# Sliding windows: partition order batch and half, alternating halves, one queue for all stores

## The chip, the cores and the metric

One core of a Trainium2 chip runs the kernel. The metric is the device time of one execution in microseconds.

## The reference

```python
batch, c, h, w = (16, 64, 64, 64)        # x, float32; window_size 8, stride 4
n_h = n_w = (64 - 8) // 4 + 1            # 15
for i in range(n_h):
    for j in range(n_w):
        result[:, i, j] = x[:, :, i*4 : i*4+8, j*4 : j*4+8]
```

The result has the shape (16, 15, 15, 64, 8, 8). Nothing is calculated: 16.78 MB are read from HBM, and 58.98 MB are written, because windows overlap by half in both directions.

## The kernel before

The rows of an image are cut into four bands of 16 (`HQ`, index q), the channels into two halves of 32 (`CH`, index ch). The whole input is held in SBUF in one tile `L`, 128 partitions by 32 channels, 16 rows and 64 columns. The partition is 32·q + 2·batch + ch.

Sixteen loads of 1 MB (line 50) fill it: four chunks of eight channels, in each the four bands, each band on 32 neighbouring partitions. Bands 0 and 1 are loaded by SP's queue, bands 2 and 3 by ACT's.

Then, for each column j of the 15 window columns and each slot s of 4 window rows in a band, VectorE gathers into a tile `g` what the four bands need for window row i = 4·q + s. For s = 0, 1, 2 the windows lie inside a band, and one copy of 128 x 2048 elements does it (line 66). For s = 3 the window's lower half is in the next band: one copy of 128 x 1024 takes the upper halves (line 68), and three copies of 32 x 1024 take the first rows of the band below, from the next 32 partitions (line 70). Then each band's 32 partitions are stored by a DMA of 256 KB (line 77), bands 0 and 1 on SP, 2 and 3 on ACT. Window row 15 doesn't exist, so SP stores 8 rows for each column and ACT 7. The pool has nine buffers for `g`. The first window (j = 0, s = 0) is made and stored in four chunks of channels.

The engines take their instructions in program order. The framework adds the waits: a copy waits for the loads that it reads, and for the stores of the buffer that it reuses; a store waits for the copies of its tile. Eight DMA completion semaphores are used in turn, so that the issue of a DMA also waits for the one that had the same semaphore, the eighth before it in the program.

Of the kernel before, what the change touches and what calls it, by code (L numbers as in the profile page):

```python
# [1 line left out]

# [4 lines left out]


@with_exitstack  # L10
def kernel(
    ctx: ExitStack,
    tc: tile.TileContext,
    x: bass.AP,
    window_size: int,
    stride: int,
    out: bass.AP,
):
    nc = tc.nc
    P = nc.NUM_PARTITIONS  # L20

    B, C, H, W = x.shape
    Bo, NH, NW, Co, WSo, WSo2 = out.shape
    WS = int(window_size)
    ST = int(stride)
    assert Bo == B and Co == C and WSo == WS and WSo2 == WS

    f32 = mybir.dt.float32

    HQ = 4  # L30
    CH = P // (B * HQ)
    CL = C // CH
    RB = H // HQ
    Q = P // HQ
    NSLOT = RB // ST
    assert Q == 32 and WS == 2 * ST

    lpool = ctx.enter_context(tc.tile_pool(name="lpool", bufs=1))
    gpool = ctx.enter_context(tc.tile_pool(name="gpool", bufs=9))


    L = lpool.tile([P, CL, RB, W], f32)
    x_v = x.rearrange("b (ch cl) (hq r) w -> hq (b ch) cl (r w)", ch=CH, hq=HQ)
    o_v = out.rearrange("b i j (ch cl) r w -> i j b ch (cl r w)", ch=CH)
    queues = [nc.sync, nc.sync, nc.scalar, nc.scalar]
    NCH = 4
    cw = CL // NCH
    for k in range(NCH):
        for q in (0, 2, 1, 3):
            queues[q].dma_start(  # L50
                out=L[q * Q : (q + 1) * Q, k * cw : (k + 1) * cw, :, :],
                in_=x_v[q, :, k * cw : (k + 1) * cw, :],
            )

    CFREE = CL * WS * WS
    for j in range(NW):
        cols = slice(j * ST, j * ST + WS)
        for s in range(NSLOT):
            g = gpool.tile([P, CL, WS, WS], f32, name="g")
            chunks = NCH if j == 0 and s == 0 else 1  # L60
            n = CL // chunks
            last = s == NSLOT - 1
            for k in range(chunks):
                cs = slice(k * n, (k + 1) * n)
                if not last:
                    nc.vector.tensor_copy(out=g[:, cs, :, :], in_=L[:, cs, s * ST : s * ST + WS, cols])  # L66
                else:
                    nc.vector.tensor_copy(out=g[:, cs, 0:ST, :], in_=L[:, cs, s * ST : RB, cols])  # L68
                    for q in range(HQ - 1):
                        nc.vector.tensor_copy(  # L70
                            out=g[q * Q : (q + 1) * Q, cs, ST:WS, :],
                            in_=L[(q + 1) * Q : (q + 2) * Q, cs, 0:ST, cols],
                        )
                for q in (0, 2, 1, 3):
                    i = NSLOT * q + s
                    if i < NH:
                        queues[q].dma_start(  # L77
                            out=o_v[i, j, :, :, k * CFREE // chunks : (k + 1) * CFREE // chunks],
                            in_=g[q * Q : (q + 1) * Q, cs, :, :],
                        )  # L80


# [1 line left out]
_INS = ['x', 'window_size', 'stride']  # L84
_OUTS = [((16, 15, 15, 64, 8, 8), 'float32')]

_NUMBERS = {'window_size': 8, 'stride': 4}


# [26 lines left out]
```

## Time and profile before

| | us |
|---|---|
| Median of 3 runs | 248.83 |
| Lowest and highest run | 240.36 and 253.69 |
| Profiled execution | 246.83 |
| Its span in the profile | 245.1 |
| VectorE busy | 96.0 |

The profile gives for each engine the busy time, and for the DMA the busy share of the 16 engines and the rate in slices of the span (40 slices of 6.13 us). q1 is SP's queue and q10 is ACT's. "SPq" and "ACTq" are the issues of DMAs on these queues. The stretches that matter here are the loads (about 2 to 55 us), the stores of both queues (62 to 219 us) and the end, in which only one queue has work. The largest waits of VectorE are for stores that have to free a buffer, 60.5 us at line 66 and 22.0 us at line 68.

### The profile page before, as it was taken

To read this page: it belongs to the slowest core of one execution; us is meant where nothing else is said; L and a number is where in the kernel's file an instruction comes from. 1 tells how busy PE (TensorE), PEld (TensorE's weight loads), DVE (VectorE), ACT (ScalarE), POOL (GpSimd) and SP (SyncE) were. 2 spreads that over 40 slices of the span, in tenths; PEclk is the share of its full clock that TensorE was granted. 3 is DMA by queue.
4 is the path that set the end of the run, shared out by engine and by line. 5 is a ranking of instruction groups with operands and counts; after the bars stand their busy time and mean duration, and the time that the engine had idled before them with its cause. 6 is when DMAs were issued, how large, how long until landed. Compare 5 with 4: busy or idle time off the path is not lost.

```text
span 245.1 us, 659 instructions
## 1 busy us (share of the span) xinstructions
DVE 96.0 (39%) x108; POOL 0.2 (0%) x4
## 2 busy tenths in 40 slices
DVE  0000000008996646453726454545555554542000
POOL 0000000000000000000000000000000000000000
DMA  6999999997999999999999999999999999999996
GB/s 212 317 320 318 318 318 320 322 326 184 326 346 314 332 321 322 330 308 328 342 333 326 322 333 338 325 338 336 308 350 350 336 345 309 326 341 272 211 210 142
DMA packets 15733, 75.82 MB, mean 309 GB/s; under 512 B 4048, under 2 KB 4048, under 8 KB 8656
## 3 DMA queue, kind: packets, MB, share of 16 engines
q1 hardware_dynamic: 8224, 39.85, 51.5%
q10 hardware_dynamic: 7504, 35.92, 43.7%
q14 instruction: 5, 0.04, 0.0%
HBM read 16.78 MB, written 58.98 MB: 309 GB/s over the span
## 4 chain that ended last, share of the span: by engine, by line
DMA 74%; DVE 7%; SPq 5%; ACTq 2%; issue 1%; DVEq 0%
DMA out_dram<-g 53%; DMA L<-in_x_dram 22%; SPq L77 5%; DVE g L70 4%; DVE g L66 3%; ACTq L77 1%; DVE g L68 1%; ACTq L50 1%; DVEq L111 0%; DVEq L66 0%; DVEq L68 0%
## 5 line engine op out<-in xcount | busy, mean ns | idle before, releaser
L66 DVE COPY g<-L 128x2048 f32<-128x2048 f32 (+1 forms) x48 | 55.1, 1159 | 103.1 <-DMA out_dram<-g 60.5
L70 DVE COPY g<-L 32x1024 f32<-32x1024 f32 x45 | 30.8, 684 | 1.1
L68 DVE COPY g<-L 128x1024 f32<-128x1024 f32 x15 | 10.4, 692 | 22.0 <-DMA out_dram<-g 22.0
L97 POOL MEMSET const-bfloat16-1.0<- 128x1 bf16 x1 | 0.1, 102 | 0.0
L97 POOL MEMSET const-uint8-127<- 128x1 uint8 x1 | 0.1, 102 | 0.0
L97 POOL MEMSET const-float32-0.0<- 128x1 f32 x1 | 0.1, 99 | 0.2 <-issue 0.2
L97 POOL MEMSET const-float32-1.0<- 128x1 f32 x1 | 0.1, 99 | 0.0
## 6 DMA issues: line engine op xcount, KB each, us to landing
out_dram<-g SPq DMA_DIRECT2D x118, 256.0 KB, 5.9
out_dram<-g ACTq DMA_DIRECT2D x103, 256.0 KB, 6.1
L<-in_x_dram SPq DMA_DIRECT2D x8, 1024.0 KB, 26.2
L<-in_x_dram ACTq DMA_DIRECT2D x8, 1024.0 KB, 26.1
out_dram<-g SPq DMA_DIRECT2D x8, 64.0 KB, 2.1
out_dram<-g ACTq DMA_DIRECT2D x8, 64.0 KB, 2.1
```

Of the source, the lines that this page charges most:

```text
L50: queues[q].dma_start(out=L[q * Q : (q + 1) * Q, k * cw : (k + 1) * cw, :, :], in_=x_v[q, :, k * cw : (k + 1) * cw, :],)
L66: nc.vector.tensor_copy(out=g[:, cs, :, :], in_=L[:, cs, s * ST : s * ST + WS, cols])
L68: nc.vector.tensor_copy(out=g[:, cs, 0:ST, :], in_=L[:, cs, s * ST : RB, cols])
L70: nc.vector.tensor_copy(out=g[q * Q : (q + 1) * Q, cs, ST:WS, :], in_=L[(q + 1) * Q : (q + 2) * Q, cs, 0:ST, cols],)
L77: queues[q].dma_start(out=o_v[i, j, :, :, k * CFREE // chunks : (k + 1) * CFREE // chunks], in_=g[q * Q : (q + 1) * Q, cs, :, :],)
L97: nc = _bacc.Bacc("TRN2", target_bir_lowering=False, num_devices=1)
```

## The change

The partition is now 64·ch + 4·batch + q: the two channel halves lie on the two halves of the partitions, and the bands of one image on neighbours.

A load takes one half, one band and eight channels: 16 partitions, every fourth one, 512 KB. All loads are on ACT's queue. The very first piece is cut in two by batches 0 to 7 and 8 to 15; after it two pieces of half 1 and two of half 0 take turns.

All stores are on SP's queue. A store of a window inside a band takes all four bands of one half at once: 64 partitions, 512 KB (`store`, line 90). A window across two bands is stored by `store_x` (line 96): 16 partitions, every fourth one, for two columns together. The windows across bands are made in a tile `gx` by one copy of 128 x 1024 (line 83) and one `stream_shuffle` of 128 x 1024 (line 84), which gives each partition the first rows of the next partition.

The order: window column 14 (`J`), slot 0 and its crossing windows are made first, and of these half 0 is stored, batches 0 to 7 and then 8 to 15. Then seven pairs of columns follow. For each pair, the crossing windows are made first; then, slot by slot, the windows of both columns are made, and half 1 is stored (two `store`, one `store_x`), then half 0. The rest of column 14 comes last. `g` has five buffers, `gx` has two, each for two columns.

```diff
-    gpool = ctx.enter_context(tc.tile_pool(name="gpool", bufs=9))
+    gpool = ctx.enter_context(tc.tile_pool(name="gpool", bufs=5))
+    xpool = ctx.enter_context(tc.tile_pool(name="xpool", bufs=2))
...
-    queues = [nc.sync, nc.sync, nc.scalar, nc.scalar]
-    for k in range(NCH):
-        for q in (0, 2, 1, 3):
-            queues[q].dma_start(
-                out=L[q * Q : (q + 1) * Q, k * cw : (k + 1) * cw, :, :],
-                in_=x_v[q, :, k * cw : (k + 1) * cw, :],
-            )
+    def load(ch, q, k, b0=0, nb=B):
+        cs = slice(k * cw, (k + 1) * cw)
+        p0 = ch * HP + b0 * HQ + q
+        nc.scalar.dma_start(
+            out=L[p0 : p0 + (nb - 1) * HQ + 1 : HQ, cs, :, :],
+            in_=x_v[ch, q, b0 : b0 + nb, cs, :],
+        )
+    pieces = [(q, k) for k in range(NCH) for q in range(HQ)]
+    load(0, *pieces[0], 0, HB)
+    load(0, *pieces[0], HB, HB)
+    for n in range(0, len(pieces), 2):
+        for u in pieces[n : n + 2]:
+            load(1, *u)
+        for u in pieces[n + 1 : n + 3]:
+            load(0, *u)
+    nxt = [min(p + 1, 31) for p in range(32)]
+    def window(j, s):
+        g = gpool.tile([P, CL, WS, WS], f32, name="g")
+        cols = slice(j * ST, j * ST + WS)
+        nc.vector.tensor_copy(out=g[:, :, :, :], in_=L[:, :, s * ST : s * ST + WS, cols])
+        return g
+    def crossing(js):
+        g = xpool.tile([P, 2, CL, WS, WS], f32, name="gx")
+        for n, j in enumerate(js):
+            cols = slice(j * ST, j * ST + WS)
+            nc.vector.tensor_copy(out=g[:, n, :, 0:ST, :], in_=L[:, :, (NSLOT - 1) * ST : RB, cols])
+            nc.vector.stream_shuffle(out=g[:, n, :, ST:WS, :], in_=L[:, :, 0:ST, cols], mask=nxt)
+        return g
+    def store(g, ch, j, s, b0=0, nb=B):
+        p0 = ch * HP + b0 * HQ
+        o = o_v[ch, s::NSLOT, j].rearrange("q b f -> b q f")[b0 : b0 + nb]
+        nc.sync.dma_start(out=o, in_=g[p0 : p0 + nb * HQ].rearrange("p c r w -> p (c r w)"))
+    def store_x(g, ch, js, q, b0=0, nb=B):
+        p0 = ch * HP + b0 * HQ + q
+        o = o_v[ch, q * NSLOT + NSLOT - 1, js[0] : js[-1] + 1].rearrange("j b f -> b j f")[b0 : b0 + nb]
+        i = g[p0 : p0 + (nb - 1) * HQ + 1 : HQ, 0 : len(js)].rearrange("p j c r w -> p j (c r w)")
+        nc.sync.dma_start(out=o, in_=i)
+    J = NW - 1
+    g0, gx = window(J, 0), crossing([J])
+    for b0 in (0, HB):
+        store(g0, 0, J, 0, b0, HB)
+        store_x(gx, 0, [J], 0, b0, HB)
+    for j in range(0, J, 2):
+        js = [j, j + 1]
+        gx = crossing(js)
+        for s in range(NSLOT - 1):
+            gs = [window(u, s) for u in js]
+            for ch in (1, 0):
+                for u, g in zip(js, gs):
+                    store(g, ch, u, s)
+                store_x(gx, ch, js, s)
+    gx = crossing([J])
+    gs = [window(J, s) for s in range(NSLOT - 1)]
+    for ch, ss in ((1, (0, 1)), (0, (1, 2)), (1, (2,))):
+        for s in ss:
+            store(gs[s], ch, J, s)
+            store_x(gx, ch, [J], s)
```

More of the change, by code (lines that the diff above doesn't have):

```diff
@@ L33 @@
     RB = H // HQ
-    Q = P // HQ
     NSLOT = RB // ST
-    assert Q == 32 and WS == 2 * ST
+    CFREE = CL * WS * WS
+    HB = B // 2
+    HP = P // CH
+    assert HQ == 4 and CH == 2 and WS == 2 * ST and HP == B * HQ
     lpool = ctx.enter_context(tc.tile_pool(name="lpool", bufs=1))
-    gpool = ctx.enter_context(tc.tile_pool(name="gpool", bufs=9))
+    gpool = ctx.enter_context(tc.tile_pool(name="gpool", bufs=5))
+    xpool = ctx.enter_context(tc.tile_pool(name="xpool", bufs=2))
     L = lpool.tile([P, CL, RB, W], f32)
-    x_v = x.rearrange("b (ch cl) (hq r) w -> hq (b ch) cl (r w)", ch=CH, hq=HQ)
@@ L44 @@
-    o_v = out.rearrange("b i j (ch cl) r w -> i j b ch (cl r w)", ch=CH)
-    queues = [nc.sync, nc.sync, nc.scalar, nc.scalar]
+    x_v = x.rearrange("b (ch cl) (hq r) w -> ch hq b cl (r w)", ch=CH, hq=HQ)
     NCH = 4
     cw = CL // NCH
-    for k in range(NCH):
-        for q in (0, 2, 1, 3):
-            queues[q].dma_start(
-                out=L[q * Q : (q + 1) * Q, k * cw : (k + 1) * cw, :, :],
-                in_=x_v[q, :, k * cw : (k + 1) * cw, :],
-            )
-    CFREE = CL * WS * WS
@@ L56 @@
-    for j in range(NW):
-        cols = slice(j * ST, j * ST + WS)
[L58 to L80, printed above, removed]
@@ new lines @@
+    o_v = out.rearrange("b i j (ch cl) r w -> ch i j b (cl r w)", ch=CH)
+    nxt = [min(p + 1, 31) for p in range(32)]
+    def window(j, s):
+        g = gpool.tile([P, CL, WS, WS], f32, name="g")
+        cols = slice(j * ST, j * ST + WS)
+        nc.vector.tensor_copy(out=g[:, :, :, :], in_=L[:, :, s * ST : s * ST + WS, cols])
[7 more added lines that the diff above has]
+        return g
```

## The prediction

> **What bounds the kernel now.** I read the busy rows first, then the rate of the transfers in stretches, then the waits.
>
> The page's first two sections show which resource is full.
>
> ```profile
> DVE 96.0 (39%) x108; POOL 0.2 (0%) x4
> DMA  6999999997999999999999999999999999999996
> GB/s 212 317 320 318 318 318 320 322 326 184 326 346 314 332 321 322 330 308 328 342 333 326 322 333 338 325 338 336 308 350 350 336 345 309 326 341 272 211 210 142
> q1 hardware_dynamic: 8224, 39.85, 51.5%
> q10 hardware_dynamic: 7504, 35.92, 43.7%
> HBM read 16.78 MB, written 58.98 MB: 309 GB/s over the span
> ```
>
> VectorE works 96 of 245.1 us; the DMA row is at nine tenths nearly throughout. So the time is bytes over rate, and the rate has levels. The last slices stand at 210 with the DMA row as full as before. The answer by stretch gives each level a figure (columns: length, DVE, POOL, clock, DMA share, GB/s):
>
> ```profile
> 2.00:55.00 53.00, 1.28 (x3) 0.00 (x0) 1.00 1.02 319
> 55.00:62.00 7.00, 5.92 (x8) 0.00 (x0) 1.00 0.80 210
> 62.00:219.00 157.00, 86.03 (x94) 0.00 (x0) 1.00 0.95 330
> 226.00:240.00 14.00, 0.00 (x0) 0.00 (x0) 1.00 0.99 210
> ```
>
> Loads take 53 us at 319, stores 157 us at 330, and the end runs at 210 with the DMA share at 0.99. Who works at the end is seen in the DMA view of that window:
>
> ```profile
> q1 hardware_dynamic: 569, 3.12, 98.6%
> out_dram<-g SPq DMA_DIRECT2D x13, 256.0 KB, 4.8
> ```
>
> Only SP's queue is left: bands 0 and 1, which lie on partitions 0 to 63. The engines aren't idle; each packet takes longer. The packet records of the trace say by how much: an 8 KB store packet takes 309 ns at its shortest, which is also the commonest value (26.5 GB/s an engine, 424 for 16); in the last 17 us nearly all take 595 to 639 ns, twice that, and one 256 KB store follows the other every 1.235 us, which is 617 ns a packet. While both queues work, the packets are a mixture, mean about 375. The completion writes of the last stores come in couples within about 20 ns of each other and keep so over 14 stores[...].
>
> [...]
>
> **The change, part by part.**
> Partition order. Partition is now 64·half + 4·batch + band. A full store takes 64 partitions of one half[...]. That is the configuration of the last 17 us of before. [...] batches 0 to 7 and then 8 to 15 of the first pieces go to engines 0 to 7 alone, and then the halves alternate in groups. So the question is how large the lead is when the alternation starts.
>
> Loads. ACT issues all 33. Engines 0 to 7 get two times 8 packets of 4 KB ahead of the rest. In before a load packet took 159 ns in the first 2 us and then mostly 200 to 205 (319 GB/s is 205). From 1.75 us, the first packet of before, the 16 packets end at 4.3 to 5.0. The third load, by before's issue spacing of 0.46 to 0.50 us, starts at about 2.7 on engines 8 to 15. Their lead is 1.6 to 2.3 us, 10 to 11 of the 16 packets of a group[...]. (10.5·205 + 5.5·309)/16 = 241 ns; if the read side runs on meanwhile, 205. I take 225. Engines 0 to 7 have 264 packets: 59.4 us, ending at 61.2. Bounds: 159 ns gives 43.7, wholly in lockstep 309 gives 83.3; before ended at 54.9. Eight transfers may be under way, so no wait is added here.
>
> Start of the stores. DVE runs in program order. It waits for all loads (0.85 us after the last packet, as in before), then copies window (14,0), 1.23; the crossing of column 14, a copy at 0.69[...]; then the crossing of columns 0 and 1, 3.8; only then window (0,0), 1.23. The four stores for engines 0 to 7 are released at 1.2 and 3.1 us after DVE's start and hold 10 packets for each of these engines. From issue to first packet 1.85 us passed at 222.5 in before, so they end at about 7. The first store for all 16 engines is released at 8.2 and begins at 10.1. By then engines 0 to 7 have been idle for 3 us: the lead is lost, whatever the shuffle costs (at the copy's 0.69 they would still be idle for about 2). The bulk begins at 61.2 + 0.85 + 10.1 = 72.1[...].
>
> Bulk. 58.98 MB less the 0.64 already stored is 58.34: 445 packets of 8 KB per engine, in groups of ten in one half. In lockstep a group takes 10·617 = 6.17 us. A small lead remains, since the engines of the first load in before began over some 0.5 us: I take one packet, 309 ns (estimate), so 9·617 + 309 = 5.86, and 44.5 groups are 261 us. No lead gives 275; two packets 247.
>
> Rest. Stores on one queue: before's unblocked issue is 0.55 us; 140 of them are 77 us, hidden behind 261 of transfers. Behind a waiting store SP has the other stores, but with eight under way the engines stay fed. [...] Buffers of 5 instead of 9 cost nothing at 6 us per group of two windows; if the stores ran at 309, a freed buffer would have about 6 us until its turn, and the copy needs about 5. The uneven end of before (15 rows of output, 8 on SP, 7 on ACT) goes away: 17 us at 210 instead of 330 were about 6 us lost.
>
> Sum: 72.1 + 261 + 1.35 (last packet to end, as before) = 334.5 of span. Before's execution had 246.83 against a span of 245.1, so 1.7 more: 336. The profiled execution is 2.0 below the median of 248.83, within the runs' 240.36 to 253.69.
>
> **The rivals.**
> The lead holds. Then every packet takes 309 and some 15 for boundaries: 44.5 groups at 3.24 are 144 us, 72.1 + 144 + 3.1 = 219, and with loads at 159 to 205, 202 to 214; I say 212. For it: packets at 309 exist in half of before's stores. Against it: DVE's order above. A group costs 6.17 − 0.308 for each packet of lead; equal to before needs a bulk of 172 us, 3.86 a group, a lead of 7.5 packets. That is the point from which it decides, worth 120 us. [...] Together 0.20.
>
> The lead grows. Noise pulls the couples apart by 3 to 6 packets: groups of 5.2 to 4.3, 268 to 307 in all, 285 in the middle. For it: the mixture in before's middle is nearer 309 than 617. Against it: the couples at the end of before keep within 20 ns. 0.13.
>
> SP's issue or DVE as the bound would need over 261 us where 77 and 84 are counted; I give it nothing of its own.
>
> **How the numbers follow.** Lockstep 0.67: 336, its own range 312 to 360 from the bounds of load, lead and group. Lead grows 0.13, lead holds or isn't needed 0.20. The range is 260 to 360; what is left out is mainly the 0.20 on the other side. A measurement of this kernel can tell about 2%. Faster 0.20, within 2% 0.02, slower 0.78.
>
> **What would show it.** Right: the GB/s row near 210 to 225 after about slice 9 with the DMA row at nine; store packets at 600 to 640; DVE waiting for stores in total over 150 us; SP's store issues lengthened. Wrong: rates of 380 or more in the stores and packets at 309, or long stretches of idle DMA, which would mean that issue or buffers bound it.

## The result, and the profile after

The changed kernel takes 322.24 us (median of 12 runs, 315.77 to 327.0), the kernel before 245.75 in the runs beside it. The ratio is 1.318, with a 95% interval of 1.304 to 1.332: slower by nearly a third. Medians are over all executions, while ratios compare only those within 1.5% of the fastest of each kernel, because other executions of both are up to 6% slower. Forecast was 336, with a range of 260 to 360. The profiled execution has 318.0 us and a span of 316.2.

These are the busy row, the two rows of slices, the queues and the bytes from the page of the changed kernel:

```profile
DVE 84.6 (27%) x94; POOL 0.2 (0%) x4
DMA  5999999952999999999999999999999999999997
GB/s 155 253 260 259 263 261 262 264 146 109 239 231 265 225 268 228 267 227 269 230 262 235 263 236 258 237 259 238 260 234 261 236 261 235 260 238 261 234 254 178
q1 hardware_dynamic: 9408, 58.99, 73.8%
q10 hardware_dynamic: 4608, 16.78, 20.8%
HBM read 16.78 MB, written 58.98 MB: 240 GB/s over the span
```

The bytes are the same, VectorE has less to do, and the DMA row is still at nine tenths. Only the rate is lower. By stretch (length, DVE, POOL, clock, DMA share, GB/s):

```profile
2.00:68.00 66.00, 0.00 (x0) 0.00 (x0) 1.00 0.99 253
70.00:80.00 10.00, 10.00 (x14) 0.00 (x0) 1.00 0.35 111
80.00:314.00 234.00, 73.90 (x81) 0.00 (x0) 1.00 0.98 247
```

The loads take 66 us at 253 GB/s, where before they took 53 at 319. The bulk of the stores takes 234 us at 247, where before there were 157 at 330 and some 24 in the end. Between them lie 10 us in which VectorE is busy throughout and the transfers aren't.

The packet records show what a low rate with a full DMA row is. Of the 8 KB store packets, 62% took 309 to 315 ns in before and 12% took 550 to 660. In the changed kernel these are 21% and 52%. Load packets of 4 KB come in two kinds, about 160 and about 316 ns, where before most took 200 to 205. The longer kind is about twice the shorter, as the 595 to 639 ns of the end of before are twice 309.

The start of the stores, from the timeline of the changed kernel (start, length, engine, line, instruction, idle before):

```profile
69.31 1.23 DVE L75 COPY g<-L 128x2048 f32<-128x2048 f32 x1 [69.31 <-DMA L<-in_x_dram]
70.56 0.83 SPq L90 DMA_DIRECT2D out_dram<-g  x1
...
73.80 0.65 SPq L96 DMA_DIRECT2D out_dram<-gx  x1
...
75.78 4.61 DVE L75 COPY g<-L 128x2048 f32<-128x2048 f32 x4
77.01 1.72 SPq L90 DMA_DIRECT2D out_dram<-g  x2
```

The four stores for eight engines are issued by 74.5 us, and their last completion writes come at 76.0. The first store for all 16 engines is issued at 77.01, and its first packets come at 78.3. The lead-in is over before there is anything to lead.

That a transfer of eight batches takes eight engines is seen in two counts of the changed kernel. The loads have 512 completion writes, 16 for each of 31 and eight for each of the two of the lead-in; the stores have 2208, 16 for each of 136 and eight for each of these four. From 2.8 to 3.9 us, with both loads of the lead-in issued, 8.1 packets are under way in the mean, so the two use the same eight engines; in the first store of the lead-in it is 8.1 too. The packet records don't name an engine: engines 0 to 7 stand here for the eight of the lead-in, 8 to 15 for the others.

How far apart the engines are is read from the completion writes, 16 for each store. In the changed kernel eight of them come together and the other eight later, by 0.9 us in the median of all stores: by 0.9 to 1.1 us for most, by about 0.4 us for each store_x. How many packets this is depends on what a packet takes meanwhile: three at 309 ns, but one and a half at 600 ns, and 52% of the store packets took 550 to 660. The time of a group says more. The stores of both halves take 236.5 us for 44.5 groups, 5.3 us each, and by the forecast's estimate (6.17 us less 0.308 for each packet of lead) this is a lead of nearly three packets of the ten that a group has. In this sense the text below speaks of three packets.

### The profile page after: what moved, and what is told of

Read it like the earlier page. It is cut to its first block, busy times and chain, and to the rows that moved or that the text cites. A ratio compares the mean times of both kernels' runs of the same rounds, so it can differ in the third digit from the quotient of the medians.

```text
span 316.2 us, 411 instructions
## 1 busy us (share of the span) xinstructions
DVE 84.6 (27%) x94; POOL 0.2 (0%) x4
## 4 chain that ended last, share of the span: by engine, by line
DMA 55%; SPq 18%; DVE 11%; issue 5%; ACTq 2%; DVEq 0%
DMA out_dram<-g 35%; DMA L<-in_x_dram 20%; SPq L96 11%; DVE g L75 9%; SPq L90 7%; DVE gx L84 2%; ACTq L54 2%; DMA out_dram<-gx 1%; DVE gx L83 0%; DVEq L75 0%; DVEq L83 0%
## 5 line engine op out<-in xcount | busy, mean ns | idle before, releaser
L75 DVE COPY g<-L 128x2048 f32<-128x2048 f32 x46 | 56.0, 1226 | 207.2 <-DMA out_dram<-g 126.4
L84 DVE STREAM_SHUFFLE gx<-L 128x1024 f32<-128x1024 f32 x16 | 20.4, 1276 | 0.0
L83 DVE COPY gx<-L 128x1024 f32<-128x1024 f32 x16 | 10.9, 680 | 0.0
```

The source lines that it names most:

```text
L75: nc.vector.tensor_copy(out=g[:, :, :, :], in_=L[:, :, s * ST : s * ST + WS, cols])
L83: nc.vector.tensor_copy(out=g[:, n, :, 0:ST, :], in_=L[:, :, (NSLOT - 1) * ST : RB, cols])
L84: nc.vector.stream_shuffle(out=g[:, n, :, ST:WS, :], in_=L[:, :, 0:ST, cols], mask=nxt)
```

## The experiments

The theory: while all engines are in one half, the rate is low, as the 210 GB/s in the end of before; it rises when engines 0 to 7 and 8 to 15 are apart by the length of a group and so in different halves; the lead-in was meant to do that, and doesn't. That the distance of these two groups decides is the author's assumption, which the profile of before doesn't show. Rivals: one queue for all stores can't do more; five buffers and the waits for them set the pace; the reads from HBM limit the loads.

**Without the lead-in.**

```diff
-    for b0 in (0, HB):
-        store(g0, 0, J, 0, b0, HB)
-        store_x(gx, 0, [J], 0, b0, HB)
+    store(g0, 0, J, 0)
+    store_x(gx, 0, [J], 0)
```

> The changed kernel with the first pieces of half 0 stored by all 16 engines (one store, one store_x) instead of batches 0 to 7 and then 8 to 15 on engines 0 to 7. Theory (the lead-in is used up before window (0,0) is ready, and the small lead left comes from the start of a transfer on the engines one after the other): the group of ten packets stays at 5.2 to 5.3 us, the whole within 2% of the changed kernel's 322 us, if anything 1 to 2 us less by the evener load. Rival (the lead-in is what gives the three packets of lead): lockstep, a group near 6.2 us, 350 to 365 us in all.

Measured: 324.0 us, against 322.24 for the changed kernel; the ratio to before is 1.322 (1.301 to 1.342). The completion writes are 0.91 us apart, as with the lead-in (0.92). As expected: the lead-in of the stores makes no difference that these runs can tell, and the three packets come from elsewhere. In the changed kernel the engines don't begin the bulk together: eight packets are under way at 78.35 us and 16 at 78.75; that the lead comes from this isn't shown.

**The lead-in beside SP's stream.**

```diff
             gs = [window(u, s) for u in js]
+            if j == 0 and s == 0:
+                g0, gj = window(J, 0), crossing([J])
+                for b0 in (0, HB):
+                    store(g0, 0, J, 0, b0, HB, nc.scalar)
+                    store_x(gj, 0, [J], 0, b0, HB, nc.scalar)
```

> The changed kernel with the same lead-in stores on ACT's queue, and their windows made after those of the first group, so that they run beside SP's stream and hold engines 0 to 7 back by ten packets whenever they come. Buffers stay at 5 and 2, all other stores stay on SP. Theory (the lead sets the rate): lead of ten packets of ten, store packets at 309 ns, groups at 3.2 to 3.9 us, bulk 145 to 175 us, 225 to 255 us in all. Rival one (one queue with its issue, whose stores take SP 1 to 2.2 us each, can't do more than about 250 GB/s) and rival two (five buffers and VectorE's waits for them set the pace): groups stay at 5.2 us, 312 to 322 us in all.

Measured: 323.73 us, a miss. The completion writes show that the lead was there for a moment: from the fourth store on, the two groups of eight came 1.50, 1.25, 1.76 and 1.85 us apart. After that they fell back to 1.24, 0.66 and then about 1.04, as in the changed kernel. At this place SP's queue ran low. The timeline of this run:

```profile
77.93 5.64 SPq L90 DMA_DIRECT2D out_dram<-g  x4
...
88.41 0.56 SPq L96 DMA_DIRECT2D out_dram<-gx  x1
```

Its waits have the same gap (who waits, for what, us in total, times, longest):

```profile
SPq L96 <- DMA out_dram<-g: 4.8, 1, 4.8
```

From 83.6 to 88.4 us SP issued nothing: a lead-in store had the semaphore that this issue needed, and took that long beside SP's stream. At 88.4 us fewer than three packets per engine were left in its queue on average, and from 88 to 90 us the DMA share is only 0.75. Some of the engines had nothing to do, probably those ahead, so the run doesn't tell whether a lead would have lasted without this gap.

**Halves alternating at each store.**

```diff
-            for ch in (1, 0):
-                for u, g in zip(js, gs):
+            for u, g in zip(js, gs):
+                for ch in (1, 0):
                     store(g, ch, u, s)
-                store_x(gx, ch, js, s)
+            for ch in (1, 0):
+                store_x(gx, ch, js, s)
```

> The changed kernel with the halves alternating at each store (groups of 4, 4, 4, 4, 2 and 2 packets) instead of after two stores and a store_x (10 packets). Theory (about three packets of lead remain whatever the order): of a group of 4 only one packet meets, (617 + 3 times 309)/4 = 386 ns a packet, bulk about 170 to 190 us, 255 to 275 us in all. Rival one (one queue) and rival two (buffers): no change, 315 to 325 us.

Measured: 281.21 us, ratio 1.153 (1.135 to 1.171): between the theory and its rivals, but far from the latter. The stretch from 95 to 215 us, in the same columns as above, first of the changed kernel and then of this run:

```profile
95.00:215.00 120.00, 42.14 (x47) 0.00 (x0) 1.00 0.98 248
95.00:215.00 120.00, 50.33 (x57) 0.00 (x0) 1.00 0.95 301
```

One queue and five buffers can do 301 GB/s; neither is what holds the changed kernel at 248. The packets took 412 ns on average, not 386. In the completion writes the groups of eight can no longer be told apart, and the store_x have only two packets for a half; how much of the difference comes from either was not measured.

**Half 0 stored through ACT's queue.** In `store` and `store_x`:

```diff
-        nc.sync.dma_start(...)
+        (nc.sync, nc.scalar)[1 - ch].dma_start(...)
```

> The changed kernel with half 0 stored by ACT's queue and half 1 by SP's; order, sizes and buffers as changed. Theory[...]: the rate of the kernel before, 320 to 350 GB/s, bulk 167 to 183 us, 250 to 270 us in all. Rival one (one queue is the limit): the same direction, and nothing tells them apart here. Rival two (buffers): no change, 315 to 325 us.

Measured: 256.08 us, ratio 1.046 (1.032 to 1.061). The same stretch:

```profile
95.00:215.00 120.00, 55.94 (x61) 0.00 (x0) 1.00 1.01 341
```

The buffers, the transfers and the bytes are those of the changed kernel. But the edit does two things at once, a second queue and one half for each queue, and this run doesn't separate them. Two of the last runs below have two queues with both halves on each, and reach 332 and 337 GB/s, so that a half for each queue isn't needed for such a rate. The second queue goes with 341 against 248 GB/s in the same stretch; how an engine divides its time between two queues isn't shown, because the packet records don't name the engine.

**The load's lead-in through SP's queue.** `load` gets the queue as a further argument, which is `nc.scalar` where none is given:

```diff
-    load(0, *pieces[0], 0, HB)
-    load(0, *pieces[0], HB, HB)
+    load(0, *pieces[0], 0, HB, nc.sync)
+    load(0, *pieces[0], HB, HB, nc.sync)
```

> The changed kernel with the first piece of half 0, batches 0 to 7 and 8 to 15, loaded through SP's queue instead of ahead of the others on ACT's; all else as changed. In the changed kernel the loads' packets are at about 160 or at about 316 ns, and last until 68.6 us. Theory (the lead of engines 8 to 15 was cut to about 6 of 16 packets because ACT took 1.29 and 0.70 us to issue the two first transfers, during which engines 8 to 15 had nothing; beside ACT's stream the 16 packets hold engines 0 to 7 back whole): load packets near 160 ns throughout, loads over at 44 to 48 us, 298 to 304 us in all. Rival (the reads from HBM can't go under the 205 ns a packet of the kernel before): loads over at 55 to 57 us, 309 to 313 us in all.

Measured: 301.02 us, ratio 1.223 (1.213 to 1.233). The last load packet ended at 51.7 us, against 68.8 in the changed kernel. Some 8 to 10 us pass until short packets prevail, and then most take 159 to 172 ns. From 2 to 42 us:

```profile
2.00:42.00 40.00, 0.00 (x0) 0.00 (x0) 1.00 1.02 344
```

The end of the loads was expected sooner, at 44 to 48; the total is within what was expected. Here a lead-in works. The reads from HBM aren't limited to the 205 ns a packet of before.

**Stores of half the size.** In `store`, two transfers of 16 channels each take the place of one of 32:

```diff
-        o = o_v[ch, s::NSLOT, j].rearrange("q b f -> b q f")[b0 : b0 + nb]
-        nc.sync.dma_start(out=o, in_=g[p0 : p0 + nb * HQ].rearrange("p c r w -> p (c r w)"))
+        for c in (0, 1):
+            h = CL // 2
+            fs = slice(c * CFREE // 2, (c + 1) * CFREE // 2)
+            o = o_v[ch, s::NSLOT, j].rearrange("q b f -> b q f")[b0 : b0 + nb, :, fs]
+            i = g[p0 : p0 + nb * HQ, c * h : (c + 1) * h].rearrange("p c r w -> p (c r w)")
+            nc.sync.dma_start(out=o, in_=i)
```

> The changed kernel with each store cut in two by channels: twice as many transfers of 64 partitions by 4 KB, store_x unchanged. In the changed kernel SP's issue of a store ends when two transfers and part of a third are left in its queue. Theory (the queue takes about three stores at a time, whatever their size, so that the leading engines can't be further ahead than what three hold, and the lead of about three packets is what is left of this): with half the bytes in three stores the lead falls to 0 to 1.5 packets of 8 KB, groups of 5.7 to 6.2 us, 340 to 362 us in all. Rival[...]: groups stay at 5.2 to 5.4 us, 318 to 328 us.

Measured: 337.38 us, ratio 1.371 (1.354 to 1.388), just under the theory's range and well over the rival's. The rate:

```profile
100.00:320.00 220.00, 66.43 (x71) 0.00 (x0) 1.00 0.96 232
```

The time is near what the theory said, but the packets don't show its reason, a lead of 0 to 1.5 packets. From 85 us on, the share of the stored bytes whose packets took at most 6% over the shortest time (309 ns for 8 KB, half of it for 4 KB) was 25%, not less than the 21% of the changed kernel. The mean time for 8 KB went from 518 to 540 ns, which with 309 ns for a short packet and 600 ns for a long one is, as an estimate, a lead of about two packets, more than the theory had; the share of the time in which an engine had a packet went from 0.98 to 0.95. So the loss is part longer packets and part time between the packets of more and smaller transfers. In the completion writes the groups of eight can no longer be told apart, so these don't measure a lead here. Whether the queue's depth sets the lead stays open.

What is seen of the depth is this. In the changed kernel an issue of 64 rows ends when 7.0 to 9.5 packets per engine are left in SP's queue, which is two whole transfers and a part of a third, and takes a median of 1.85 us, against about 0.6 for the first ones into an empty queue. With half-size stores some 8 to 10 packets of 4 KB were left (the middle half of the issues), not much over half the bytes. ACT's loads, in contrast, had 46 to 52 packets per engine waiting from the ninth on and took 0.56 us each to issue. So the load queue had room for engines that are far apart, and the store queue for less.

**Both working edits together, and then without the gap.** The first joins the load's lead-in through SP with the two store queues:

> Both edits that are each meant to keep the halves apart: the load's lead-in through SP's queue, and half 0 stored through ACT's queue, half 1 through SP's. Theory: the sum of the two, 256 less the 21 to 24 us of the loads, 232 to 236 us, under the kernel before at 245.5. Rival (loads at 205 ns a packet): 243 to 246 us.

Measured: 237.16 us, ratio 0.956 (0.944 to 0.968): under the kernel before.

The second drops the lead-in of the stores and makes the windows first (the lines that the loop replaces are left out here, and the queues are as in the run before):

```diff
     J = NW - 1
...
+    for js in [[j, j + 1] for j in range(0, J, 2)] + [[J]]:
+        for s in range(NSLOT - 1):
+            gs = [window(u, s) for u in js]
+            if s == 0:
+                gx = crossing(js)
+            for ch in (1, 0):
+                for u, g in zip(js, gs):
+                    store(g, ch, u, s)
+                store_x(gx, ch, js, s)
```

> As the last one, with column 14 stored like the others at the end instead of half of its slot 0 first, and in each pair the windows of slot 0 made before the crossing windows, so that the first store for all engines waits for one copy after the loads instead of eight VectorE instructions. Theory (with two queues no lead has to be made; the gap between the loads and the bulk of the stores is DVE's order): about 6 us less than the last one, 226 to 230 us. Rival (the first stores are needed for the halves to be apart): the stores lose their 340 GB/s, and it is 10 us or more slower than the last one.

Measured: 226.84 us, ratio 0.921 (0.914 to 0.929), the best of all. Its timeline after the loads:

```profile
52.87 2.36 DVE L75 COPY g<-L 128x2048 f32<-128x2048 f32 x2 [52.87 <-DMA L<-in_x_dram]
54.13 1.95 SPq L90 DMA_DIRECT2D out_dram<-g  x2
54.13 1.72 ACTq L90 DMA_DIRECT2D out_dram<-g  x2
```

The first store for all engines comes 1.3 us after VectorE's start, not 7.7, and the rate stays up:

```profile
95.00:215.00 120.00, 54.10 (x58) 0.00 (x0) 1.00 1.01 358
```

Against the kernel before, this one differs in the loads, the size of the stores, the partition order and the even end. How its 8% divide among these was not separated.

**A lead that the queue can hold.** Three more runs asked whether the stores can have a lead at all if it is short: halves alternate at each store of four packets, and two stores of 16 KB per engine to engines 0 to 7 are meant to hold these back by just one group. Of the edit only the new stores are shown:

```diff
...
+            if j == 0 and s == 1:
+                g0 = window(J, 0)
+                for b0 in (0, HB):
+                    store(g0, 0, J, 0, b0, HB, 0, CL // 2, nc.scalar)
...
```

With store_x through ACT's queue, first with the two stores, then without them, then with them and the load's lead-in through SP:

> A lead that SP's queue can hold. SP stores only transfers of four packets per engine and changes the half at each; all store_x go through ACT's queue; column 14 comes at the end, except that half 0 of its slot 0, channels 0 to 15, goes through ACT's queue to engines 0 to 7 alone in two stores during the first pair of columns: 32 KB per engine, the length of one group. Loads as changed. Theory (a lead as long as a group, and shorter than what three stores hold, keeps the halves apart with the other stores still on one queue): most of SP's packets at 309 ns, the bulk at 340 to 380 GB/s, 228 to 245 us in all, clearly under the same kernel without the two stores. Rival (one queue for the stores, or what three stores hold, caps the rate whatever the lead): no difference between the two, 255 to 280 us both.

> The same with half 0 of column 14's slot 0 stored at the end by all 16 engines, so without a lead-in. Theory: a lead of two to three of the four packets forms by itself, as where the halves alternated at each store on one queue (281 us), and the store_x beside it help a little: 245 to 270 us, 10 us or more above the one with the lead-in. Rival: the same time as with it.

> The kernel with the small lead, and the load's lead-in through SP's queue as well. Theory: the loads end at 45 to 48 instead of 68.6 us, so 20 to 23 us less than the kernel with the small lead alone: 206 to 224 us, at or under the best so far (226.8). Rival (the lead is lost in the stores): 232 to 258 us.

Measured: 256.78, 255.27 and 236.97 us, where before had 246.06. There is no difference between the first two, so the rival is right about them: the two stores do nothing. Their stretches from 76 to 250 us, in this order:

```profile
76.00:250.00 174.00, 78.50 (x87) 0.00 (x0) 1.00 0.99 332
76.00:250.00 174.00, 79.43 (x89) 0.00 (x0) 1.00 0.99 337
```

Here both queues store both halves, and the rate is near the 341 of the run with a half for each queue. The third is 20 us less, which is again the loads: VectorE starts at 53.2 us, not 72.5. It was expected at 206 to 224 us, lies in the range of its rival and doesn't reach 226.84. In the first run the completion writes of a store were spread evenly over 1.3 to 2.4 us, with no groups of eight.

With store_x on SP's queue too:

> The same small lead-in as in the last group of runs, but with every other store on SP, store_x too (in runs of four packets in a half where they come in pairs)[...]. Halves alternate at each store; windows of slot 0 are made before the crossing windows. Theory (a lead of one group, held by a queue of three stores): most packets at 309 ns, bulk at 370 to 410 GB/s, 226 to 242 us. Rival (the leads on the store queue settle by themselves and a lead-in doesn't last): the rate of the run in which the halves alternated at each store, about 300 GB/s, less some 5 us for the shorter start: 266 to 280 us.

Measured: 275.78 us, ratio 1.129 (1.115 to 1.143), at 304 GB/s from 95 to 215 us: the rival again. The expected gain of a lead in the stores showed in no run. That the engines of the changed kernel keep apart by themselves, by 0.9 us in the completion writes, and that a lead put in beside the stream brings nothing (323.73 us), is what was seen. Only the run with the larger lead-in shows such a lead for a moment; in the two with the small one no groups of eight appear in the completion writes, so that it isn't known whether a lead was ever there. Why three packets form was not found.

## Why the prediction was right, point by point

- **The mechanism.** Right, as far as the record reaches. All engines in one half at the same time give a full DMA row at a low rate, as the 210 GB/s in the last 17 us of before: 52% of the store packets took 550 to 660 ns, about twice the shortest 309, and the same transfers with the halves mixed, in another order or on two queues, ran at 301 and 341 GB/s instead of 248. Why one half is slower isn't shown: the trace doesn't name the engine of a packet, and a limit of the half as a whole would look the same here as engines that hinder each other.
- **Start of the stores.** Right. From DVE's start to the first store for all engines 8.2 us were forecast, 7.7 passed. The forecast's price of the shuffle, which is in the 8.2 us and in the 84 us of VectorE, was an assumption, as before has no shuffle; here one of 128 x 1024 took 1.28 us, the crossing windows of columns 0 and 1 took 3.6 (72.24 to 75.88) where 3.8 were forecast, and VectorE was busy for 84.6. The gap from the last load to the bulk's first packets was forecast as 10.95 us and measured as 9.5 (68.8 to 78.3).
- **The lead lost there.** The fact is right: the lead-in's last completion writes come 2.3 us before the bulk's first packets. The reason may be too narrow. Making the windows earlier need not have been enough, since in the runs with a lead-in beside the stream there was no gain either, though once with a gap in SP's issues.
- **Loads.** Forecast to end at 61.2 us, ended at 68.8. The term that failed is "before's issue spacing of 0.46 to 0.50 us": ACT took 1.29 and 0.70 us for the first two transfers of every fourth partition, so the third was issued at 2.8 instead of 1.7 us. With the first packet at 2.3 us, the 16 packets of 159 ns end at 4.9; the third transfer's first packets come at 4.0 to 4.4, which leaves a lead of at most 0.9 us, six packets instead of 10 to 11. Ten of 16 at the longer time give, as an estimate, (10·316 + 6·160)/16 = 258 ns, and the mean of the load packets is 255.
- **Bulk.** Forecast 261 us, measured 236.5 (78.3 to 314.8). The term that failed is the lead of "one packet": it was about three. By the same rule, 6.17 − 0.308·3 = 5.25 us a group and 44.5 groups are 233 us. A smaller part is the price of a long packet, 617 ns in the forecast, while the packets over 550 ns had a median of 598 here. In the last 14 stores of before themselves it is rather 1.26 us from store to store, or 630 ns a packet, than the 1.235 us of the forecast.
- **Sum.** The loads are 7.6 us over, the bulk 24.5 under, and the gap 1.5 under; 336 less 18 is the 318.0 of the profiled execution. That the total came so near is in part luck, because the two larger errors have opposite signs.
- **Signs.** The rate was forecast at 210 to 225 and is 225 to 269; DVE's waits for stores were forecast over 150 us and are 126.4. A longer lead than forecast would give both. SP's issues lengthened as forecast.

```profile
DVE g L75 <- DMA out_dram<-g: 126.4, 36, 7.3
```

- **The rival that the lead grows** described the direction of the error. Its range for a group, 4.3 to 5.2 us, ends just under the 5.3 that was measured, while the main case had 5.9. By the bulk alone, the result is nearest to this rival's edge; the late loads brought the total back towards the main case. Its reason, slow noise, was not seen: the two groups of eight were 0.6 us apart in the first two stores and 1.1 us after the first change of half, and stayed there.

The end of before, counted as 6 us lost, was not tried by itself.

## What to carry to other kernels

A full DMA row says that the engines are occupied, not that they move much: here a share of 0.98 went with 248 GB/s, and one of 0.95 with 330 in before. Compare the packet's time with its shortest (518 against 309 ns here), and ask which half of the partitions the transfers of one moment have in common. An arrangement that lives on two groups of engines being apart has to keep the distance by itself. Behind the lead-in through SP's queue most load packets took 159 to 172 ns, and the load queue of the changed kernel had some 50 packets per engine waiting; the stores, with 7 to 9.5, kept no lead, though that the depth is the reason isn't shown. Alternating the halves more often went with 301 GB/s instead of 248, and a second queue with 341, or with 358 without any lead-in of the stores. Before a first transfer is given a special place, look at what the next one waits for on the engine that makes its data.

## What the runs showed of the hardware

- Loads mostly at 159 to 172 ns for 4 KB, 344 GB/s from 2 to 42 us, where the kernel before had mostly 200 to 205 ns and 319 GB/s: the reads can go faster than in before.
- A store queue whose issue ends with two transfers and part of a third waiting, 7.0 to 9.5 packets of 8 KB per engine, while the load queue held up to six and a half transfers, 46 to 52 packets of 4 KB per engine; the completion writes go to eight semaphores in the trace.
- Two queues with opposite halves of the partitions at 341 to 358 GB/s, two queues with both halves on each at 332 to 337, one queue at 248 to 304 depending on how often the half changes.
- Issues of loads to every fourth partition: 1.29 and 0.70 us for the first two, about 0.62 for the next, 0.56 later; loads to neighbouring partitions 0.39 to 0.47 at first and 0.31 later.
